# A 31-tap depthwise convolution on VectorE, written as three half-length filters on even and odd tokens

## The chip, the cores and the metric

The kernel runs on one core of one Trainium2 chip. The metric is the device time of one execution in microseconds (us), the median of several. Before the change it is 2021.61 us, the median of three runs (2020.27 to 2026.67).

## What is computed

The program is one step of a two-layer decoder trunk for 528 prompt tokens (16 learned ones and 512 given ones) and 8 sample tokens. Each layer is FFN, mixer, FFN, each with a root-mean-square norm ahead of it; the first layer's mixer is a convolution branch beside windowed attention, the second's a state-space scan. The change lies in the convolution branch, for the prompt tokens alone. Cut to that, the reference is:

```python
z = proj[..., o3:o4] * jax.nn.sigmoid(proj[..., o4:])          # 512 channels
zf = jnp.concatenate([ctx, z], axis=1)                         # 30 rows of zeros, then 528 tokens
y = lax.conv_general_dilated(zf, conv_w[:, None, :], (1,), 'VALID',
                             feature_group_count=C_CONV) + conv_b   # 31 taps for each channel
c_out = silu(layernorm(y, ln_g, ln_b))                         # over the 512 channels
out = jnp.concatenate([a_out, c_out], axis=-1) @ w_out         # a_out: the attention's output
```

## The kernel before

Channels lie on the 128 partitions and tokens along the free dimension; all is 32-bit. A tile of 536 columns holds two halves of 268: 264 prompt tokens and 4 sample tokens each. Every matrix product is done in three passes with high and low parts (`whi`, `wlo` of the weights, `xh`/`xl` or `mh`/`ml` of the operand), so a product with K blocks of 128 is 3 x K x 2 matmuls of 268 columns, and each block of weights costs a copy on ScalarE (L128) and a subtraction on VectorE (L129).

The mixer (`_mixer0`, from L508) has 512 convolution channels in four groups c = 0 to 3. For each, `z_tile(c)` computes the gated input with two products and leaves it in `zp[c]`, 30 zeros and then 528 tokens. `conv(c)` then multiplies `zp[c]`, shifted by j, with the weight column of tap j and adds it into `yc[c]`, one VectorE instruction of 528 columns for each tap (L573 the first, L575 the others). Group 3 is special: its first 8 taps (`NPE`) are done on TensorE as products with diagonal matrices (`conv_pe`, L587 to L594) into an accumulator `self.pc`; VectorE does the other 23, and L799 adds `self.pc` in. Each group has a `yc[c]` of its own and no other scratch.

When all four are there, `norm(h)` does the layer norm over channels for each half h: the mean by four products with a constant matrix (L778), the subtraction (L782), squares on ScalarE (L784), four products (L785), a reciprocal square root with one correction step (`rsqrt`, L297 to L302), the scaling (L790), Silu with scale and bias (L791) and the split into `mh[4+c]`, `ml[4+c]` (L148, L149). `project` then applies the output weights in two sweeps over eight groups d of output channels: first the attention half (24 matmuls for each d, L139 and L142, and the addition into `x[d]` on VectorE, L832), then the convolution half (24 more, L841). The next FFN follows.

The order on each engine is not the order of the text. A scheduler with a model of the chip's timing takes instructions in the text's order of priority as soon as what they read and the tiles they write are to be had, and so fills one step's gaps with another's work. A tile of a pool with `bufs=n` is given out anew when the last use of an older one in the text is over. The accumulators named `mm` (`acc2`) are two; `self.pc` is one of them, from `conv_pe` until L799 has read it.

Of the kernel before, what the change touches and what calls it, by code (L numbers as in the profile page):

```python
# [12 lines left out]
AF = mybir.ActivationFunctionType  # L13
OP = mybir.AluOpType
# [6 lines left out]
NP = 528  # L21
HP = 264
HT = 268
# [3 lines left out]
NCK = 66  # L27
NEG = -1e9
ORDER0 = "z0 k v q0 a0 z3 q1 a1 c0 z1 q2 a2 q3 z2 l s a3".split()
NCV, NPE = 3, 8  # L30
LOENG = lambda nc: nc.vector
SLOTS = dict(P1=0, P2=1, P6=3, P5=5, P7=6, P4=9, P3=11)
CHUNKS = ((0, 6), (6, 8), (14, 8))
WHOLE, HEAD = 3, tuple((d,) for d in range(8))
ORDER1 = [(a[0], int(a[1])) for a in
          "U0 U1 U2 U3 X0 X1 U4 X2 Y0 U5 X3 T0 U6 Y1 X4 T1 Y2 X5 T2 U7 Y3 X6 T3 Y4 Y5 X7 T4 Y6 T5 Y7 T6 T7".split()]

# [1 line left out]
def halves(ap):  # L39

    return ap.rearrange("p (h t) -> p h t", h=2)


def pv(ap):

    return halves(ap)[:, :, :HP]
# [7 lines left out]
def h2(ap):  # L54

    return ap.rearrange("p (h t) -> p h t", h=2)
# [6 lines left out]
class Trunk:  # L63
# [467 lines left out]
    def _mixer0(self, p, stage):  # L531
        nc, io, out, ident = self.nc, self.io, self.out, self.ident
        R = halves(self.R[:])
        win = io["ab_w_in"][0].rearrange("(k p) f -> p k f", p=128)
        cos, sin, perm, gmask, sel, maskb, mask4, identb, sk, sk4, sks, o512, cw, zs, sc, kcT, vc = (
            self.m0[n] for n in "cos sin perm gmask sel maskb mask4 identb sk sk4 sks o512 cw zs sc kcT vc".split())

        def tl(shape, name, dt=F32, bufs=1):
            return p.tile(shape, dt, name=name, bufs=bufs)

        wcol = lambda c, j: cw[:, c * 31 + j:c * 31 + j + 1]
        vcol = lambda i, c: cw[:, 124 + 4 * i + c:124 + 4 * i + c + 1]


        zp = [tl([128, 30 + NP], f"zp{c}") for c in range(4)]
        yc = [tl([128, NT], f"yc{c}") for c in range(4)]
# [18 lines left out]
            nc.vector.scalar_tensor_tensor(sv(yc[c][:]), zn, wcol(c, 30), sc[:, c].rearrange("p (h b) -> p h b", h=2),  # L565
                                           op0=OP.mult, op1=OP.add)

        def conv(c, hs=(0, 1), j0=0):
            y = halves(yc[c][:])[:, hs[0]:hs[-1] + 1, :HP]
            for j in range(j0, 31):  # L570
                z = h2(zp[c][:, j:j + NP])[:, hs[0]:hs[-1] + 1]
                if j == j0:
                    nc.vector.tensor_scalar(y, z, wcol(c, j), vcol(0, c), op0=OP.mult, op1=OP.add)  # L573
                else:
                    nc.vector.scalar_tensor_tensor(y, z, wcol(c, j), y, op0=OP.mult, op1=OP.add)  # L575

        def conv_pe(i):

# [195 lines left out]
        def norm(h):  # L774
            hc = slice(h * HT, (h + 1) * HT)
            pm = self.bank()[:, :HT]
            for c in range(4):
                nc.tensor.matmul(pm, o512[:], yc[c][:, hc], start=c == 0, stop=c == 3)  # L778
            pq = self.bank()[:, :HT]
            for c in range(4):  # L780
                y = yc[c][:, hc]
                nc.vector.tensor_sub(y, y, pm)  # L782
                s = self.work("ta")[:, :HT]
                nc.scalar.activation(s, y, AF.Square)  # L784
                nc.tensor.matmul(pq, o512[:], s, start=c == 0, stop=c == 3)  # L785
            rl = self.R[:, hc]
            self.rsqrt([rl], [pq])
            for c in range(4):
                y = yc[c][:, hc]
                nc.vector.tensor_mul(y, y, rl)  # L790
                nc.scalar.activation(y, y, AF.Silu, scale=vcol(1, c), bias=vcol(2, c))  # L791
                self.put(self.mh[4 + c][:, hc], self.ml[4 + c][:, hc], y)

        for c in range(WHOLE):
            conv(c)
        if NPE < 31:
            conv(3, j0=NPE)
            y = pv(yc[3][:])
            nc.vector.tensor_add(y, y, self.pc[:, :, :HP])  # L799
        else:  # L800
            nc.scalar.activation(pv(yc[3][:]), self.pc[:, :, :HP], AF.Identity, bias=vcol(0, 3))
        for h in range(2):
            for c in range(WHOLE, NCV):
                conv(c, (h,))
            norm(h)

        pz = self.bank()
# [657 lines left out]
```

## Time and profile before

| | before |
|---|---|
| median of 3 runs | 2021.61 us |
| the profiled execution | 2020.43 us |
| its span, first to last instruction | 2018.6 us |
| TensorE busy, mean granted clock | 1933.7 us, 0.984 |
| VectorE busy | 1577.0 us |
| ScalarE busy | 938.1 us |

Busy time counts an instruction from its start to its end; matmuls overlap, so a full busy time says only that TensorE was never empty. How many matmuls were done in a stretch, and the granted clock beside them, say more. A row of the timeline that merges several instructions gives the start of the first and the time from there to the end of the last.

### The profile page before, as it was taken

What the parts mean: (1) busy time and instruction counts of PE and PEld (TensorE: products, weight loads), DVE (VectorE), ACT (ScalarE), POOL (GpSimd) and SP (SyncE); (2) the same over time, 40 slices, a digit from 0 to 9 for tenths busy, and PEclk for the clock granted to TensorE, in tenths of its full rate; (3) what the DMA queues carried; (4) which work ended last, traced back from release to release, by engine and by line L of the source; (5) the groups of instructions that cost most, each with busy time, mean ns of one, the idle gap of its engine ahead of it and who ended that gap; (6) DMA issues with size and microseconds to landing.
All of it is one profiled execution on the core that took longest, in us unless ns stands there. A gap on an engine that the chain in (4) does not pass through costs nothing.

```text
span 2018.6 us, 37789 instructions
## 1 busy us (share of the span) xinstructions
PE 1933.7 (96%) x15338; PEld 1870.4 (93%) x15338; DVE 1577.0 (78%) x2799; ACT 938.1 (46%) x1639; POOL 81.4 (4%) x160
## 2 busy tenths in 40 slices
PE   6999999999999899999999999999989999999998
PEld 5999999998779899898999999999989999999997
DVE  5768769678868999989789997696694486794876
ACT  5535435434446635435465354354324364452543
POOL 2000000000000000020001210000110000000000
PEclk9899999999989999999999999999999999999999
DMA  6233333321005234353334543236583323333231
GB/s 185 81 107 87 95 95 95 116 75 44 27 22 123 65 94 127 121 156 113 102 94 120 163 130 103 86 102 193 164 261 101 90 63 95 95 111 89 84 105 53
DMA packets 372066, 213.51 MB, mean 106 GB/s; under 512 B 36299, under 2 KB 362503, under 8 KB 371869
## 3 DMA queue, kind: packets, MB, share of 16 engines
q1 hardware_dynamic: 354901, 190.63, 32.8%
q0 software_dynamic: 6432, 19.40, 3.0%
q10 hardware_dynamic: 10560, 1.09, 0.4%
q8 instruction: 120, 1.97, 0.4%
q14 instruction: 53, 0.43, 0.1%
HBM read 193.14 MB, written 23.65 MB: 107 GB/s over the span
## 4 chain that ended last, share of the span: by engine, by line
PE 73%; DVE 14%; DMA 5%; issue 4%; ACT 3%; ACTq 0%; POOL 0%; SPq 0%; DVEq 0%; POOLq 0%
PE mm L266 25%; PE mm L139 18%; PE mm L142 9%; PE S L139 7%; PE S L266 4%; PE S L142 4%; DMA raw<-in_ffn_w_gu 3%; DVE wlo L225 2%; PE S L747 1%; ACT whi L128 1%; DVE ml L149 1%; DVE wlo L129 1%; DVE ql L225 1%; DMA pb<-in_x_prompt 1%; DVE raw L229 1%
## 5 line engine op out<-in xcount | busy, mean ns | idle before, releaser
L224 ACT ACTIVATE whi<-raw 128x1024 fp32r<-128x1024 f32 (+1 forms) x237 | 216.9, 916 | 184.1 <-PE mm L266 50.5
L128 ACT ACTIVATE whi<-raw 128x1024 fp32r<-128x1024 f32 (+2 forms) x166 | 159.6, 973 | 303.3 <-PE mm L139 156.7
L139 PE MATMUL mm<-mh,whi 128*128 128x268 f32 x1224 | 262.1, 291 | 5.9 <-ACT whi L128 3.0
L225 DVE TENSOR_TENSOR wlo<-raw,whi 128x1024 fp32r<-128x1024 f32 (+1 forms) x237 | 246.7, 1041 | 25.5 <-ACT whi L224 24.7
L139 PE MATMUL mm<-ml,whi 128*128 128x268 f32 x1224 | 259.5, 287 | 0.1
L142 PE MATMUL mm<-mh,wlo 128*128 128x268 f32 x1224 | 259.5, 288 | 0.1
L129 DVE TENSOR_TENSOR wlo<-raw,whi 128x1024 fp32r<-128x1024 f32 (+2 forms) x166 | 184.5, 1117 | 70.1 <-ACT whi L128 67.7
L139 PEld LDWEIGHTS mm<-mh,whi 128*128 128x128 f32 x1224 | 194.5, 190 | 10.6 <-ACT whi L128 4.1
L142 PEld LDWEIGHTS mm<-mh,wlo 128*128 128x128 f32 x1224 | 194.5, 189 | 1.6 <-DVE wlo L129 1.2
L139 PEld LDWEIGHTS mm<-ml,whi 128*128 128x128 f32 x1224 | 194.9, 189 | 0.7 <-DVE ml L149 0.4
L266 PE MATMUL mm<-xh,whi 128*128 128x268 f32 x632 | 183.6, 291 | 5.9 <-ACT sn L274 5.3
L266 PE MATMUL mm<-eh,wlo 128*128 128x268 f32 x632 | 181.5, 287 | 3.2 <-DVE wlo L225 3.2
L266 PE MATMUL mm<-eh,whi 128*128 128x268 f32 x632 | 182.4, 289 | 1.8 <-ACT whi L224 1.1
L266 PE MATMUL mm<-xh,wlo 128*128 128x268 f32 x632 | 181.0, 286 | 0.0
L266 PE MATMUL mm<-xl,whi 128*128 128x268 f32 x632 | 180.8, 286 | 0.0
L266 PE MATMUL mm<-el,whi 128*128 128x268 f32 x632 | 180.6, 286 | 0.0
L266 PEld LDWEIGHTS mm<-xh,whi 128*128 128x128 f32 x632 | 119.0, 188 | 10.6 <-ACT sn L274 9.6
L139 PE MATMUL S<-mh,whi 128*128 128x268 f32 x568 | 121.3, 289 | 3.0 <-ACT mh L148 1.6
L266 PEld LDWEIGHTS mm<-eh,wlo 128*128 128x128 f32 x632 | 118.8, 188 | 4.2 <-DVE wlo L225 4.0
L266 PEld LDWEIGHTS mm<-eh,whi 128*128 128x128 f32 x632 | 119.1, 188 | 3.6 <-ACT whi L224 1.6
L142 PE MATMUL S<-mh,wlo 128*128 128x268 f32 x568 | 120.1, 287 | 0.3 <-DVE wlo L129 0.3
L266 PEld LDWEIGHTS mm<-xl,whi 128*128 128x128 f32 x632 | 119.1, 189 | 0.0
(520 smaller groups left out, 5079.7 us busy)
## 6 DMA issues: line engine op xcount, KB each, us to landing
raw<-in_ffn_w_gu SPq DMA_DIRECT2D x174, 512.0 KB
raw<-in_ffn_w_down SPq DMA_DIRECT2D x64, 512.0 KB
raw<-in_ffn_w_down SPq DMA_DIRECT2D x32, 384.0 KB
raw<-in_ssm_w_glu SPq DMA_DIRECT2D x16, 512.0 KB
raw<-in_ab_w_in SPq DMA_DIRECT2D x10, 512.0 KB
dB<-B POOLq DMA_DIRECT2D x16, 256.0 KB, 2.9
dC<-Z POOLq DMA_DIRECT2D x32, 128.0 KB, 3.2
dT<-dK POOLq DMA_DIRECT2D x8, 512.0 KB, 5.0
```

The lines of the kernel that those rows point to most:

```text
L128: nc.scalar.activation(hi[:, :K], raw[:, :K], AF.Copy)
L129: nc.vector.tensor_sub(lo[:, :K], raw[:, :K], hi[:, :K].bitcast(F32))
L139: nc.tensor.matmul(ps[:, h, :HT], hi[:, k, :], src[:, h * HT:(h + 1) * HT], start=(k == 0 and i == 0), stop=False)
L142: nc.tensor.matmul(ps[:, h, :HT], lo[:, k, :], xh[k][:, h * HT:(h + 1) * HT], start=False, stop=(k == K - 1))
L149: nc.vector.tensor_sub(lo, src, hi.bitcast(F32))
L224: nc.scalar.activation(h, r, AF.Copy)
L225: nc.vector.tensor_sub(l, r, h.bitcast(F32))
L229: nc.vector.tensor_add(U[:, k0], U[:, k0], G[:, k0])
L266: nc.tensor.matmul(ps, w[:, c + k, :], b[k], start=bool(first and k + i == 0), stop=bool(last and k == 3 and i == 2), skip_group_check=True)
L747: nc.tensor.matmul(S[:, g, :w], qT[t][rw, 128 * b:128 * b + 128], kT[rw, k0:k0 + w], start=False, stop=True)
```

## The change

Even and odd outputs are computed apart. With z1 the odd tokens, d0 = even - odd and d1 = next even - odd, the 31-tap sum for the even outputs is S + (16 taps on d0), for the odd ones S + (15 taps on d1), where S is 16 taps on z1 with the sums of neighbouring weights (`ws`). Each of the three filters runs on 264 columns. For a group that is two subtractions, 16 + 16 + 15 instructions in place of 31; for group 3, whose first 8 taps stay on TensorE, 12 + 12 + 11 in place of 23. `z1` is read with a step of two elements, and the last instruction of each phase writes `yc[c]` with a step of two. S and the running sum y lie in the two halves of `self.sq`, a tile that the norms of the FFNs use and that is free here; d0 and d1 are one tile each. All four groups use the same S, y, d0 and d1. `conv(3)` stands last in the text, as before.

```diff
-NCV, NPE = 3, 8
+NPE = 8
-WHOLE, HEAD = 3, tuple((d,) for d in range(8))
+HEAD = tuple((d,) for d in range(8))
...
-        def conv(c, hs=(0, 1), j0=0):
-            y = halves(yc[c][:])[:, hs[0]:hs[-1] + 1, :HP]
-            for j in range(j0, 31):
-                z = h2(zp[c][:, j:j + NP])[:, hs[0]:hs[-1] + 1]
-                if j == j0:
-                    nc.vector.tensor_scalar(y, z, wcol(c, j), vcol(0, c), op0=OP.mult, op1=OP.add)
+        ws = tl([128, 4, 16], "ws")
+        cwv = cw[:, :124].rearrange("p (c j) -> p c j", c=4)
+        nc.vector.tensor_add(ws[:, :, :15], cwv[:, :, 0:30:2], cwv[:, :, 1:31:2])
+        nc.vector.tensor_copy(ws[:, :, 15], cwv[:, :, 30])
+
+        def conv(c, j0=0):
+
+            z, n, i0 = zp[c], HP + 15, j0 // 2
+            d0, d1 = (tl([128, n], name)[:] for name in ("d0", "d1"))
+            z1 = z[:, 1:2 * n:2]
+            S, y = self.sq[:, :HP], self.sq[:, HT:HT + HP]
+            nc.vector.tensor_sub(d0, z[:, 0:2 * n:2], z1)
+            nc.vector.tensor_sub(d1[:, :n - 1], z[:, 2:2 * n:2], z1[:, :n - 1])
+            for i in range(i0, 16):
+                w = ws[:, c, i:i + 1]
+                if i == i0:
+                    nc.vector.tensor_scalar(S, z1[:, i:i + HP], w, vcol(0, c), op0=OP.mult, op1=OP.add)
                 else:
-                    nc.vector.scalar_tensor_tensor(y, z, wcol(c, j), y, op0=OP.mult, op1=OP.add)
+                    nc.vector.scalar_tensor_tensor(S, z1[:, i:i + HP], w, S, op0=OP.mult, op1=OP.add)
+            for p, (d, last) in enumerate(((d0, 15), (d1, 14))):
+                o = halves(yc[c][:])[:, :, p:HP:2]
+                for i in range(i0, last + 1):
+                    a, b, t = d[:, i:i + HP], y if i > i0 else S, y
+                    if i == last:
+                        a, b, t = h2(a), h2(b), o
+                    nc.vector.scalar_tensor_tensor(t, a, wcol(c, 2 * i + p), b, op0=OP.mult, op1=OP.add)
...
-        for c in range(WHOLE):
+        for c in range(3):
             conv(c)
...
```

What is left out are branches that were not taken and the same calls in other words. In the changed kernel L582 and L583 write d0 and d1, L587 and L589 are the taps of S, L596 the taps of the two phases, L819 the addition of `self.pc`; L803 to L812 are the norm, L848 and L857 the additions into `x[d]`.

The first place is VectorE, from the last taps of group 3 to the first of group 1. Before (`yc3` is group 3, `mm_5389` is `self.pc`, `zp1` the input of group 1):

```order
L575 SCALAR_TENSOR_TENSOR yc3_4629<-zp3_4625,cw_1467,yc3_4629 128x2x264
L560 SCALAR_TENSOR_TENSOR ta_5558<-mm_5448,R_117 128x536
L575 SCALAR_TENSOR_TENSOR yc3_4629<-zp3_4625,cw_1467,yc3_4629 128x2x264
L562 SCALAR_TENSOR_TENSOR zp1_4623<-tb_5559,ta_5558 128x528
L564 SCALAR_TENSOR_TENSOR zs_1574<-tb_5559,ta_5558 128x8
L129 TENSOR_TENSOR wlo_5813<-raw_5811,whi_5812 128x1024
L666 TENSOR_REDUCE st_5368<-S_5361 128x2
L149 TENSOR_TENSOR ml1_110<-ms_5324,mh1_102 128x128
L575 SCALAR_TENSOR_TENSOR yc3_4629<-zp3_4625,cw_1467,yc3_4629 128x2x264
L573 TENSOR_SCALAR yc1_4627<-zp1_4623,cw_1467 128x2x264
L565 SCALAR_TENSOR_TENSOR yc1_4627<-zs_1574,cw_1467,sc_1575 128x2x4
L799 TENSOR_TENSOR yc3_4629<-yc3_4629,mm_5389 128x2x264
```

Group 3 is done, and `self.pc` read, as group 1 begins. In the changed kernel VectorE has no tap of group 3 there; these are the end of group 2 and of group 3 in it, with the additions of the attention half's products (L848) between the taps (`mm_5392` is `self.pc`):

```order
L596 SCALAR_TENSOR_TENSOR yc2_4628<-d1_6240,cw_1467,sq_118 128x2x132
L583 TENSOR_TENSOR d1_6291<-zp3_4625 128x278
L596 SCALAR_TENSOR_TENSOR sq_118<-d0_6290,cw_1467,sq_118 128x264 x3
L848 TENSOR_TENSOR x2_79<-mm_6504,x2_79 128x536
...
L596 SCALAR_TENSOR_TENSOR sq_118<-d1_6291,cw_1467,sq_118 128x264 x3
L596 SCALAR_TENSOR_TENSOR yc3_4629<-d1_6291,cw_1467,sq_118 128x2x132
L848 TENSOR_TENSOR x6_83<-mm_6636,x6_83 128x536
L819 TENSOR_TENSOR yc3_4629<-yc3_4629,mm_5392 128x2x264
L129 TENSOR_TENSOR wlo_6739<-raw_6737,whi_6738 128x512
L803 TENSOR_TENSOR yc0_4626<-yc0_4626,ms_6330 128x268
```

Group 3 now comes last, behind group 2, whose S, y, d0 and d1 it takes over, and seven of the eight additions of the attention half stand ahead of L819.

The second place is TensorE, in the attention half of the projection. Before, with `mm_6359` and `mm_6392` the accumulators of d = 0 and d = 1:

```order
L139 MATMUL mm_6359<-mh0_101,whi_6361 128x268 x2
L139 MATMUL mm_6392<-mh0_101,whi_6394 128x268 x2
L139 MATMUL mm_6359<-ml0_109,whi_6361 128x268 x2
L142 MATMUL mm_6359<-mh0_101,wlo_6362 128x268 x2
L139 MATMUL mm_6359<-mh1_102,whi_6361 128x268 x2
L139 MATMUL mm_6392<-ml0_109,whi_6394 128x268
```

Two of them are open at once. After, `mm_6438`, `mm_6471` and `mm_6504` are d = 0, 1 and 2:

```order
L799 MATMUL ms_6330<-yc1_4627,o512_1275 128x268
L139 MATMUL mm_6438<-mh3_104,whi_6440 128x268
L139 MATMUL mm_6438<-ml3_112,whi_6440 128x268 x2
L142 MATMUL mm_6438<-mh3_104,wlo_6441 128x268 x2
L139 MATMUL mm_6471<-mh0_101,whi_6473 128x268 x2
...
L142 MATMUL mm_6471<-mh3_104,wlo_6474 128x268 x2
L139 MATMUL mm_6504<-mh0_101,whi_6506 128x268 x2
```

One product is finished before the next begins, for all eight d, and the products of the mean (L799, L778 before) stand among them: those of group 3's `yc` behind the last.

## Rows read from the trace of the kernel before

**Rows 1.** Page, busy time, share of the span and instructions
```profile
PE 1933.7 (96%) x15338; PEld 1870.4 (93%) x15338; DVE 1577.0 (78%) x2799; ACT 938.1 (46%) x1639; POOL 81.4 (4%) x160
```
**Rows 2.** Windows: start:end, length, busy (x count) of PE PEld DVE ACT POOL, PEclk
```profile
410.00:430.00 20.00, 20.00 (x161) 19.86 (x160) 13.06 (x22) 9.07 (x12) 0.00 (x0) 1.00 0.31 79
510.00:541.00 31.00, 31.00 (x228) 27.07 (x226) 25.89 (x49) 11.12 (x35) 0.00 (x0) 1.00 0.11 31
541.00:587.00 46.00, 39.56 (x210) 26.82 (x210) 37.17 (x79) 20.36 (x75) 0.00 (x0) 0.70 0.02 7
587.00:618.00 31.00, 30.89 (x223) 29.12 (x222) 22.14 (x51) 21.42 (x40) 0.55 (x1) 1.00 0.23 64
618.00:643.00 25.00, 22.33 (x166) 21.90 (x166) 19.53 (x45) 15.20 (x25) 0.00 (x0) 0.93 0.77 158
```
**Rows 3.** Tile yc: durations in ns (min/median/max), first and last start
```profile
L575 DVE SCALAR_TENSOR_TENSOR yc<-zp,cw,yc x112: 744/760/771, 433.6 to 582.3; 128x528 f32<-128x528 f32 x112
L784 ACT ACTIVATE ta<-yc x8: 411/414/429, 589.2 to 605.3; 128x268 f32<-128x268 f32 x8
L148 ACT ACTIVATE mh<-yc x8: 408/410/413, 603.3 to 617.2; 128x268 fp32r<-128x268 f32 x8
L149 DVE TENSOR_TENSOR ml<-yc,mh x8: 426/433/439, 603.7 to 617.9; 128x268 fp32r<-128x268 f32 x8
L799 DVE TENSOR_TENSOR yc<-yc,mm x1: 693/693/693, 509.8 to 509.8; 128x528 f32<-128x528 f32 x1
```
**Rows 4.** Timeline, VectorE: taps of one group; a chain of 268 columns
```profile
488.56 2.37 DVE L575 SCALAR_TENSOR_TENSOR yc<-zp,cw,yc 128x528 f32<-128x528 f32 x3
610.03 0.44 DVE L300 SCALAR_TENSOR_TENSOR tb<-ms,tb 128x268 f32<-128x268 f32 x1
610.50 0.30 DVE L301 TENSOR_SCALAR tb<-tb 128x268 f32<-128x268 f32 x1
```
**Rows 5.** Timeline: one accumulator handed on between the two products of group 1
```profile
493.29 0.37 PE L142 MATMUL mm<-xh,wlo 128*128 128x268 f32 x1
493.81 0.70 DVE L557 TENSOR_TENSOR tb<-mm,R 128x536 f32<-128x536 f32 x1
494.57 0.63 PE L139 MATMUL mm<-xh,whi 128*128 128x268 f32 x2
```
**Rows 6.** Critical chain: a tap in it; attention's last product, the first mean
```profile
558.49 0.72 DVE yc L575
585.99 0.67 PE ms L761 x8
586.66 2.00 PE ms L778 x8
```
**Rows 7.** Timeline: an addition into x and a low part of weights
```profile
607.80 0.72 DVE L832 TENSOR_TENSOR x<-mm,x 128x536 f32<-128x536 f32 x1 [0.38 <-PE mm L142]
608.43 0.68 DVE L129 TENSOR_TENSOR wlo<-raw,whi 128x512 fp32r<-128x512 f32 x1
```
**Rows 8.** Timeline, ScalarE in the norm
```profile
609.04 0.49 ACT L297 ACTIVATE ta<-ms,eps 128x268 f32<-128x268 f32 x1
609.43 0.57 ACT L811 ACTIVATE ta<-ms 30x512 f32<-30x512 f32 x1
612.36 1.28 ACT L791 ACT_TABLE_LOAD   x1
613.66 1.11 ACT L791 ACTIVATE yc<-yc,cw 128x268 f32<-128x268 f32 x2
```
**Rows 9.** Timeline: the convolution half, half-clock matmuls, the FFN's first
```profile
625.29 0.63 ACT L128 ACTIVATE whi<-raw 128x512 fp32r<-128x512 f32 x1 [7.73 <-DMA craw<-in_ssm_c_re]
628.35 0.43 PE L142 MATMUL mm<-mh,wlo 128*128 128x268 f32 x1
628.57 0.42 PE L139 MATMUL mm<-mh,whi 128*128 128x268 f32 x1
642.94 0.42 PE L139 MATMUL S<-xh,whi 128*128 128x268 f32 x2
```

More of the change, by code (lines that the diff above doesn't have):

```diff
@@ L792, in norm @@
                 self.put(self.mh[4 + c][:, hc], self.ml[4 + c][:, hc], y)
-        for c in range(WHOLE):
+        for c in range(3):
             conv(c)
[L796 to L801, printed above, removed]
+        conv(3, j0=NPE)
+        y = pv(yc[3][:])
+        nc.vector.tensor_add(y, y, self.pc[:, :, :HP])
         for h in range(2):
-            for c in range(WHOLE, NCV):
-                conv(c, (h,))
             norm(h)
```

## The prediction

> **What bounds the kernel now.** The page comes first: TensorE is busy for 96% of the span, VectorE for 78% [rows 1]. So a microsecond saved on VectorE counts only where TensorE waits for it. Next comes the place of the convolution: its taps start between 433.6 and 582.3 us [rows 3], inside a mixer that ends, for this purpose, when the next FFN's first matmul starts at 642.94 [rows 9]. The windows cut that stretch into stages [rows 2]. To 541, TensorE does 228 matmuls in 31 us at full clock; in the undisturbed stretch 410 to 430 it does 161 in 20, that is 0.124 us for one of 268 columns. From 541 to 587 it does 210 in 46 us at a mean granted clock of 0.70: the last attention heads are a chain over three engines. From 587 to 618 it is full again, at clock 1.00: it does the attention half of the projection while VectorE and ScalarE do the norm. That is the cover that the change touches. Here the convolution is over in time: the last tap starts at 582.3, and attention's last product is followed at 586.66, without a gap, by the products of the mean [rows 6]. The norm's last low part starts at 617.9 and takes 0.43 [rows 3].
>
> **The price of a tap.** Three taps of one group in a row take 2.37 us; with 0.76 for the last, that is 0.80 from start to start, since each needs the sum that the one before it wrote [rows 3, 4]. For 264 columns the nearest rows are a dependent chain of 268: 0.44 us for one, 0.47 from start to start [rows 4]. An input with a step of two elements appears in no row; bounds are 0.44 (as the dense row) and 0.80 (as if the skipped columns were read too). I take 0.47, the row of the same width. Then a group of 31 taps goes from 30 x 0.80 + 0.6 = 24.6 us to (47 + 2) x 0.47 = 23.0, group 3 from 22 x 0.80 + 0.6 = 18.2 to (35 + 2) x 0.47 = 17.4. Together VectorE saves 3 x 1.6 + 0.8 = 5.6 us, for 21% fewer columns but 58% more instructions in a group of 31 (49, with the two subtractions). The two instructions for `ws` are of 60 and 4 columns; they stand in the first FFN, where TensorE is full, and I cost them at nothing (0.5 us if it were not).
>
> [...]
>
> **What moves, and the wait that this adds.** Before, the four groups had nothing in common, so group 3's taps ran early beside group 0's, and L799 released `self.pc` at 509.8 + 0.69 = 510.5 [rows 3]. Now all groups share S, y, d0 and d1, and group 3 stands last in the text. So it waits for group 2, whose input is the last that TensorE delivers. Two things follow.
>
> First, `self.pc` keeps one of the two `mm` accumulators for some 100 us longer. Each product there must then wait until VectorE has emptied the one before. Such a handing on stands in the trace from when both kernels have one: the last matmul starts at 493.29, the VectorE instruction at 493.81, the next product at 494.57 [rows 5], so 1.28 us from start to start instead of 0.124, some 1.15 lost where no attention work fills it. In q2, q3 and z2 attention does fill it, except for about 2 us behind q2 (two VectorE instructions, a product, two more), with 1 us for the rest: 3 us.
>
> Against this stand the attention's waits. A tap in front of a small instruction holds it up; one such tap is a piece of 0.72 us of the chain that ended last [rows 6]. With 0.44 in place of 0.76, the mean wait behind a tap falls by 0.16; over some 20 VectorE steps of the last heads that is 3 us, and group 3's 17 us no longer compete earlier. Also some 5 us of attention's products move ahead of z2's end as filler, and leave the tail. I take attention's end 3 us earlier, at 583.7, with bounds of 7 us earlier (all waits shrink) and 1 us later (the handing on is not filled).
>
> **The norm loses its cover.** Behind attention's last product VectorE's order still has 43 tap and subtraction instructions ahead of L819, with 7 additions into x (0.71), 6 low parts (0.68) and L819 itself (0.69): 43 x 0.47 + 5.0 + 4.1 + 0.7 = 30.0 us [rows 3, 4, 7]. Some of the taps alternate between two groups and may run closer, at 0.40 by the ratio of width, which gives 27. TensorE needs about as long for the attention half: 24 x 0.124 = 3.0 us for each d, then 0.38 + 0.72 + 0.1 for the addition [rows 7], 4.2 us together, some 26 for the six and a bit that L819 waits for. So L819 ends at about 583.7 + 30 = 613.7, and by then the attention half is all but done.
>
> Only now can the last product of the mean be made, and the norm runs with TensorE nearly empty. To its first reciprocal root it takes 5.9 us: a product (0.5), a subtraction, the squares, with the second half's four products (2.0, as [rows 6]) queued ahead of the last two products of the squares. From there ScalarE works without a gap: 4 squares 1.5, table load 1.28, three Silu and a copy and a Silu 2.6, table load 1.28, root 0.49, two evacuations 1.2, three copies 1.2, table load 1.28, four Silu with four copies 3.8, which is 14.6 [rows 3, 8]. So the norm's last part is in place at 613.7 + 20.5 = 634.2. Before it was at 618.3. If each hand-over costs 0.3 us more than I have put, it is 24 instead of 20.5; 18 if the halves overlap better.
>
> From there to the FFN's first matmul was 24.6 us before: ScalarE issues the transfers for the state-space weights, which holds the next weights' copy up by 7.73 us, then come five d of 24 matmuls, some at half clock (0.22 us from start to start) [rows 9]. ScalarE's queue is the same here, so I leave the 24.6 as it is, and the first FFN matmul comes at 658.8 in place of 642.9.
>
> **Sum.** The delay is 30.0 + 20.5 - (618.3 - 586.7) = +18.9, less 3 for attention's end: +16. Nothing behind changes. On the profiled execution's 2020.43 (span 2018.6 and 1.8 around it) that is 2036.4; the median before is 1.2 above the profiled one, so 2037.6, say 2038.
>
> **Rivals.**
> *The clock falls as well.* Before, 587 to 618 was at clock 1.00 and 541 to 587, with its sparse matmuls, at 0.70 [rows 2]. [...] Against it: before, the engine also fell there, and 166 matmuls still fit into the 25 us from 618. At the full price it gives 2056; I give 0.15 to more than 2048.
> *The step of two is not free.* If the taps on z1 take 0.80, the 12 of group 3 and what is left of group 2 cost 12 x 0.33 = 4 us behind attention and some 5 before: 2045. For it speaks only that no row shows such a read; 0.07. [...]
> *The delay is absorbed.* Attention ends 7 us early, the taps behind it run at 0.40 and the norm in 18: 27 + 18 - 31.6 - 7 = +6, and a little more gives no change (within 0.3%, 6 us, about what a measurement of this kernel tells from none): 2024. For it: VectorE was busy for 37.2 of the 46 us of the tail [rows 2]. 0.13.
> *Faster.* If short taps free the attention tail itself, the place is 541 to 587: VectorE would have to finish groups 2 and 3 before attention ends, which decides from the point where under 8 us of taps are left behind it. Then the old cover is whole again, the tail gains 3 to 7 us and the time is 2016. Against it is the order, which puts 43 tap instructions behind attention's last. That the change doesn't do what it says, and VectorE gains nothing at all, belongs to the forecast, which rests on 5.6 us hardly at all. 0.05.
>
> **How the numbers follow.** The forecast has 0.60, its own range 2030 to 2045: +9 to +24 from the bounds of attention's end, of the taps left (27 to 30) and of the norm (18 to 24). With the rivals, 8 in 10 lie between 2025 and 2050. Faster 0.05; same 0.13; slower 0.60 + 0.15 + 0.07 = 0.82.
>
> **What will show it.** L589 and L596 at 0.43 to 0.45 us each; L819 near 613 where L799 was at 509.8; gaps of about 1.2 us between the attention half's products; a window of some 20 us behind L819 with few matmuls; the last L149 of the norm near 634, the FFN's first matmul near 659; the same distance from there to the end. It is wrong if L819 comes before 600, or if the norm ends within 7 us of 618.

## The result, and the profile after

The changed kernel takes 2048.45 us (median of four runs, 2045.68 to 2051.08) where the kernel before takes 2022.09 (2020.27 to 2026.67): 1.0125 times as long (95% interval 1.0104 to 1.0147), and the two medians are 26.4 us apart. The forecast was slower, 2038, with a range of its own of 2030 to 2045: the direction came, and the time lies 3 us above that range. The profiled execution took 2050.56 us with a span of 2048.6, 30.0 above the span of before, at a mean granted clock of 0.983 against 0.984. Page, busy time:

```profile
PE 1940.6 (95%) x15338; PEld 1874.4 (91%) x15338; DVE 1578.4 (77%) x2869; ACT 940.5 (46%) x1639; POOL 81.8 (4%) x160
```

VectorE has 70 instructions more than in [rows 1] and is busy 1.4 us longer, not 5.6 us less. Groups of VectorE's instructions from 430 to 612 us: line, operation, tiles and shapes, count, busy us, mean ns, idle before:

```profile
L596 DVE SCALAR_TENSOR_TENSOR sq<-d,cw,sq 128x264 f32<-128x264 f32 x108 | 52.8, 489 | 1.7
L589 DVE SCALAR_TENSOR_TENSOR sq<-zp,ws,sq 128x264 f32<-128x264 f32 x56 | 27.3, 488 | 0.8
L583 DVE TENSOR_TENSOR d<-zp 128x278 f32<-128x278 f32 x4 | 1.8, 443 | 0.0
```

A short tap takes 0.49 us, with a dense input (L596) as with one read in steps of two (L589). Tile `yc`, the rows that answer to [rows 3]:

```profile
L596 DVE SCALAR_TENSOR_TENSOR yc<-d,cw,sq x8: 485/494/496, 461.9 to 608.0; 128x264 f32<-128x264 f32 x8
L149 DVE TENSOR_TENSOR ml<-yc,mh x8: 427/430/439, 624.8 to 634.6; 128x268 fp32r<-128x268 f32 x8
L819 DVE TENSOR_TENSOR yc<-yc,mm x1: 693/693/693, 609.5 to 609.5; 128x528 f32<-128x528 f32 x1
```

The addition of `self.pc`, at 509.8 before, starts at 609.5; the norm's last low part, at 617.9 before, at 634.6. The windows, against [rows 2]:

```profile
510.00:541.00 31.00, 27.75 (x202) 21.36 (x200) 26.52 (x62) 13.64 (x42) 0.00 (x0) 1.00 0.07 18
590.00:620.00 30.00, 24.20 (x159) 21.42 (x159) 22.13 (x45) 7.67 (x14) 0.00 (x0) 0.98 0.20 57
620.00:650.00 30.00, 22.80 (x134) 20.36 (x133) 17.90 (x49) 20.92 (x38) 0.55 (x1) 0.83 0.43 73
```

From 590 to 620 TensorE does 159 matmuls; before it did 223 in the 31 us from 587. ScalarE is busy for 7.7 us of these 30: until the last group is summed it has only copies of weights to do. TensorE's timeline in that stretch:

```profile
576.42 1.13 PE L782 MATMUL ms<-pT,vtok 128*64 128x128 f32 x8 [0.69 <-ACT pT L777]
577.48 2.16 PE L799 MATMUL ms<-yc,o 128*128 128x268 f32 x4
...
597.41 0.48 PE L139 MATMUL mm<-mh,whi 128*128 128x268 f32 x2 [0.90 <-DVE x L848]
601.53 0.48 PE L139 MATMUL mm<-mh,whi 128*128 128x268 f32 x2 [0.90 <-DVE x L848]
605.64 0.48 PE L139 MATMUL mm<-mh,whi 128*128 128x268 f32 x2 [0.90 <-DVE x L848]
609.76 0.48 PE L139 MATMUL mm<-mh,whi 128*128 128x268 f32 x2 [0.90 <-DVE x L848]
...
612.70 0.61 PE L799 MATMUL ms<-yc,o 128*128 128x268 f32 x2
...
614.29 1.17 PE L806 MATMUL ms<-ta,o 128*128 128x268 f32 x4 [0.86 <-ACT ta L805]
...
658.78 0.42 PE L139 MATMUL S<-xh,whi 128*128 128x268 f32 x2
```

Attention's last product starts at 576.42. From 593 on each d of the attention half takes 4.1 us and begins only when VectorE has added the one before into `x` (the bracket: 0.90 us idle, released by L848). VectorE in its turn waits for the product that it is to add, since the addition stands between the taps in its order:

```profile
592.43 0.72 DVE L848 TENSOR_TENSOR x<-mm,x 128x536 f32<-128x536 f32 x1 [1.90 <-PE mm L142]
596.55 0.72 DVE L848 TENSOR_TENSOR x<-mm,x 128x536 f32<-128x536 f32 x1 [0.41 <-PE mm L142]
```

Seven of the eight products are added ahead of L819. The eighth, from 609.76, holds the norm up: the mean's last products (L799), which L819 releases at 610.2, stand behind it on TensorE and start at 612.70. Behind 614 TensorE has little to do but the norm's own products. The FFN's first matmul comes at 658.78, 15.84 later than in [rows 9].

### The profile page after: what moved, and what is told of

It is laid out like the page before. It is cut to its first block, busy times and chain, and to the rows that moved or that the text cites. A ratio compares the mean times of both kernels' runs of the same rounds, so it can differ in the third digit from the quotient of the medians.

```text
span 2048.6 us, 37878 instructions
## 1 busy us (share of the span) xinstructions
PE 1940.6 (95%) x15338; PEld 1874.4 (91%) x15338; DVE 1578.4 (77%) x2869; ACT 940.5 (46%) x1639; POOL 81.8 (4%) x160
## 4 chain that ended last, share of the span: by engine, by line
PE 74%; DVE 14%; DMA 5%; issue 4%; ACT 3%; ACTq 0%; DVEq 0%; POOL 0%; SPq 0%
PE mm L266 24%; PE mm L139 19%; PE mm L142 9%; PE S L139 8%; PE S L266 4%; PE S L142 4%; DMA raw<-in_ffn_w_gu 3%; DVE wlo L225 2%; PE S L768 1%; DVE ml L149 1%; ACT whi L128 1%; DVE wlo L129 1%; DVE ql L225 1%; DVE tb L286 1%; DMA pb<-in_x_prompt 1%
## 5 line engine op out<-in xcount | busy, mean ns | idle before, releaser
L225 DVE TENSOR_TENSOR wlo<-raw,whi 128x1024 fp32r<-128x1024 f32 (+1 forms) x237 | 246.9, 1042 | 26.4 <-ACT whi L224 25.2
L139 PE MATMUL S<-ml,whi 128*128 128x268 f32 x568 | 119.7, 287 | 0.0
## 6 DMA issues: line engine op xcount, KB each, us to landing
raw<-in_ffn_w_down SPq DMA_DIRECT2D x32, 384.0 KB
```

What stands on the lines that cost most here:

```text
L139: nc.tensor.matmul(ps[:, h, :HT], hi[:, k, :], src[:, h * HT:(h + 1) * HT], start=(k == 0 and i == 0), stop=False)
L225: nc.vector.tensor_sub(l, r, h.bitcast(F32))
```

## The experiments

Each stands beside runs of the kernel before on the same chip: 2019.95 us (17 runs) for the first four, 2021.61 (7 runs) for the others. All are given in one table at the end of this section.

**The changed kernel again**, unchanged.

> The changed kernel once more, for a second trace of the same instruction order. Theory A (the delay is made in the mixer and by the other order that the scheduler chose up to 1009 us; behind that both kernels have the same order and the rest is scatter): the FFN's first matmul again within 1.5 us of 658.8, and the stretch from the second rstd (1071.8 in the first trace) to the end within 3 us of the kernel before, so the first trace's 7 us there are scatter. Rival (something lasting, such as the clock, makes the later stages longer in the changed kernel): the 7 us come again.

2050.38 us, ratio 1.0147 (1.0126 to 1.0168), span 2049.3. The loss repeats, and its places do too: the FFN's first matmul at 660.38, 0.1 us outside the 1.5 that were expected. From the norm of the next FFN to the end it takes 976.2 us, after 976.8 in the first trace and 970.8 in the kernel before: the excess there comes again, as the rival had it, and the theory of scatter fails. (The kernel before, profiled again below, has 975.4 there.) Attention's last product moved from 576.42 to 579.90 between the two executions, so about 3 us of it is chance.

**Group 3 second in the text**, with the new taps and the shared scratch kept.

```diff
-        for c in range(3):
-            conv(c)
+        conv(0)
         conv(3, j0=NPE)
         y = pv(yc[3][:])
         nc.vector.tensor_add(y, y, self.pc[:, :, :HP])
+        conv(1)
+        conv(2)
```

> The changed kernel with group 3 and the addition of self.pc second in the text (0, 3, 1, 2 in place of 0, 1, 2, 3), all else the same: the same 184 instructions, the same shared scratch. Theory A (group 3's place behind group 2 costs the time): no taps behind attention, L819's counterpart near 510 to 520, the norm's last low part at 616 +- 5, the FFN's first matmul at 641 +- 5, the whole 2014 to 2026. Rival B (more and shorter instructions on VectorE cost it, wherever they stand): 2040 or more. Rival C (half of the loss is the scheduler's other order behind the mixer, which has nothing to do with group 3): 2028 to 2038.

2023.79 us, 12 runs, ratio 1.0011 (0.9998 to 1.0025): the loss is gone. Tile `yc` in it:

```profile
L149 DVE TENSOR_TENSOR ml<-yc,mh x8: 426/434/439, 602.7 to 616.9; 128x268 fp32r<-128x268 f32 x8
L818 DVE TENSOR_TENSOR yc<-yc,mm x1: 696/696/696, 517.4 to 517.4; 128x528 f32<-128x528 f32 x1
```

With all 184 short instructions in place, but `self.pc` added at 517.4, the norm ends at 617.3, a microsecond before [rows 3]. The new form itself costs nothing that can be measured, and it gives nothing.

**The old taps with a shared sum.** The kernel before, with the running sum of all four groups in `self.sq` and only the last tap writing `yc[c]`.

```diff
+            s = pv(self.sq[:])
...
-                    nc.vector.scalar_tensor_tensor(y, z, wcol(c, j), y, op0=OP.mult, op1=OP.add)
+                    nc.vector.scalar_tensor_tensor(s if j < 30 else y, z, wcol(c, j), s, op0=OP.mult, op1=OP.add)
```

> The kernel before with its own taps of 528 columns, but with the running sum of all groups in one tile (self.sq), the last tap of each group writing its yc: 116 tap instructions as before, group 3 behind group 2 as in the changed kernel. Theory A: slower, as the changed kernel; 29 taps of 0.80 are left behind attention, 23 us, with 10 us of other VectorE work: the FFN's first matmul at 655 to 665, the whole 2036 to 2052. Rival B (the shorter taps cost the time): within 6 us of the kernel before.

2047.60 us, ratio 1.0138 (1.0121 to 1.0156): the whole loss, without one short tap. Its `yc`:

```profile
L576 DVE SCALAR_TENSOR_TENSOR yc<-zp,cw,sq x4: 769/769/772, 477.1 to 611.3; 128x528 f32<-128x528 f32 x4
L149 DVE TENSOR_TENSOR ml<-yc,mh x8: 428/432/439, 626.0 to 635.9; 128x268 fp32r<-128x268 f32 x8
L800 DVE TENSOR_TENSOR yc<-yc,mm x1: 705/705/705, 612.1 to 612.1; 128x528 f32<-128x528 f32 x1
```

**The held accumulator given back.** The changed kernel, with `self.pc` copied by ScalarE into `ml[7]` right behind `conv_pe` and added from there; that copy has the type of the high parts (`fp32r`), and the low part of group 3's first 8 taps is left out.

```diff
+            nc.scalar.activation(pv(self.ml[7][:]), self.pc[:, :, :HP], AF.Copy)
...
-        nc.vector.tensor_add(y, y, self.pc[:, :, :HP])
+        nc.vector.tensor_add(y, y, pv(self.ml[7][:].bitcast(F32)))
```

> The changed kernel with self.pc copied out of its accumulator by ScalarE as soon as it is complete (into a tile that is free until the norm, in the rounded 32-bit format of the high parts, so the low bits of group 3's first 8 taps are lost), and added from there at the end. Both accumulators are free from about 485 us on; group 3 still comes last. Theory A1 (the late group 3 itself and the norm without cover are the cause): the gaps between the attention half's products go, but the norm's last part comes at 628 to 636 and the whole is 2036 to 2049. Rival A2 (the held accumulator is the cause): within 8 us of the kernel before.

2047.83 us, ratio 1.0129 (1.0106 to 1.0151). The loss stays; the norm's last low part comes 2.0 us earlier:

```profile
L149 DVE TENSOR_TENSOR ml<-yc,mh x8: 427/432/440, 622.7 to 632.6; 128x268 fp32r<-128x268 f32 x8
L820 DVE TENSOR_TENSOR yc<-yc,ml x1: 709/709/709, 607.4 to 607.4; 128x528 f32<-128x528 f32 x1
```

The gaps do go: a d now takes 2.97 us instead of 4.12, as VectorE's additions show.

```profile
593.35 0.72 DVE L849 TENSOR_TENSOR x<-mm,x 128x536 f32<-128x536 f32 x1 [0.32 <-PE mm L142]
596.32 0.72 DVE L849 TENSOR_TENSOR x<-mm,x 128x536 f32<-128x536 f32 x1 [0.32 <-PE mm L142]
```

But attention's last product starts at 583.20, 3 to 7 us later than in the two profiles of the changed kernel, and the norm's last low part comes only 2.0 us earlier than in the first of them and 4.1 earlier than in the second. So the accumulator's longer life is worth some 2 to 4 us there, not the loss.

**Group 3 alone in the old form**, in its place at the end of the text; groups 0 to 2 keep the new form.

```diff
             z, n, i0 = zp[c], HP + 15, j0 // 2
+            if c == 3:
+                y = halves(yc[c][:])[:, :, :HP]
...
+                        nc.vector.scalar_tensor_tensor(y, z, wcol(c, j), y, op0=OP.mult, op1=OP.add)
+                return
```

> The changed kernel, with group 3's 23 taps on VectorE in the old form: 528 columns each, summed in yc[3], without the shared S, y, d0 and d1; groups 0 to 2 keep the new form, and the text's order is unchanged. Theory A (the time is lost because group 3 has to wait for group 2's scratch, so that the norm comes behind the attention half): group 3 is done early again, self.pc is read before 530 us, the norm's last low part is in place at 615 to 620, the next FFN's first matmul at 640 to 645, and the time is that of the kernel before, 2016 to 2027. Rival B (the many short instructions of groups 0 to 2 cost the time, wherever group 3 stands): 139 of the 174 short taps are still there, so most of the loss stays: 2038 or more.

2017.46 us, ratio 0.9990 (0.9966 to 1.0015), no change. Group 3 needs nobody's scratch and the scheduler takes it early, though it stands last in the text; tile `yc` and the window against the one above:

```profile
L585 DVE SCALAR_TENSOR_TENSOR yc<-zp,cw,yc x22: 755/760/769, 468.5 to 506.4; 128x528 f32<-128x528 f32 x22
L149 DVE TENSOR_TENSOR ml<-yc,mh x8: 426/434/439, 601.4 to 615.5; 128x268 fp32r<-128x268 f32 x8
L605 DVE SCALAR_TENSOR_TENSOR yc<-d,cw,sq x6: 473/484/494, 462.2 to 583.6; 128x264 f32<-128x264 f32 x6
L828 DVE TENSOR_TENSOR yc<-yc,mm x1: 700/700/700, 508.3 to 508.3; 128x528 f32<-128x528 f32 x1
```
```profile
590.00:620.00 30.00, 29.89 (x231) 28.96 (x230) 21.53 (x58) 19.31 (x35) 0.55 (x1) 1.00 0.37 84
```

231 matmuls in the 30 us in which the changed kernel does 159. That is the cover, back again. (The expectation miscounts: with the first tap of each sum there are 176 short taps in the changed kernel, and 141 of them are left here; its two theories stay apart all the same.)

**Fewer taps in the last place.** `conv(3, j0=28)` in place of `conv(3, j0=NPE)` in the changed kernel: taps 8 to 27 of group 3 are left out.

> The changed kernel with the taps 8 to 27 of group 3 left out, so that group 3 issues 5 tap instructions and 2 subtractions on VectorE instead of 35 and 2; it still comes last and shares the scratch. 30 instructions of 0.50 us are 15 us less between attention's end and L819. Theory A: L819 ends near 595 instead of 610, and the norm's last low part is in place at 618 to 622 instead of 635, the FFN's first matmul near 644. From there two theories part. If what is lost later (14 us of the 30 in the profiled executions: 6 to 8 in the two FFNs behind, 4 in the state-space mixer, 2 at the end) comes with a late mixer, it goes as well: 2020 to 2028. If it comes with the changed code itself, it stays: 2031 to 2037.

2030.23 us, ratio 1.0047 (1.0024 to 1.0071), where the changed kernel has 1.0125 and 1.0147, each against the kernel before on its own chip: 16 to 20 us less, for 15 us of work taken from that place.

```profile
L149 DVE TENSOR_TENSOR ml<-yc,mh x8: 430/436/439, 611.7 to 624.2; 128x268 fp32r<-128x268 f32 x8
L819 DVE TENSOR_TENSOR yc<-yc,mm x1: 692/692/692, 592.2 to 592.2; 128x528 f32<-128x528 f32 x1
```

L819 comes 17.3 us earlier, the last low part 10.4: the norm now takes 31.7 us behind L819, since its products share TensorE with the attention half again (215 matmuls from 590 to 620 us). The time, 2030, is just below the range of the theory in which the later loss stays (2031 to 2037) and above that in which it goes (2020 to 2028): some of it stays. The table says where.

**The kernel before again.**

> The kernel before, unchanged, for a second profile of it. The state-space mixer took 198.0 us in the first profile of it and 197.8 in the kernel with group 3 second, but 201.8 to 203.8 in the four kernels with a late norm, with the same instructions in the same order and short stretches at half clock in it. If the half clock there comes with the late norm: 198 again and one stretch at most. If it is chance from one execution to the next: any value from 198 to 204. The time is 2012 to 2026.

2022.78 us, one run. The state-space mixer takes 202.4 us in it instead of 198.0. Windows of 60 us, from 37.3 us behind the start of that mixer, in the kernel before, in this run of it, and in the changed kernel, in that order:

```profile
1473.90:1533.90 60.00, 52.34 (x540) 50.28 (x540) 50.05 (x104) 20.45 (x40) 6.23 (x17) 0.97 0.73 215
```
```profile
1471.00:1531.00 60.00, 51.21 (x500) 49.08 (x501) 49.89 (x104) 18.46 (x36) 6.31 (x17) 0.91 0.70 209
```
```profile
1500.00:1560.00 60.00, 51.41 (x504) 49.48 (x505) 49.96 (x104) 19.06 (x37) 6.42 (x17) 0.91 0.70 210
```

The first profile of the kernel before had a granted clock of 0.97 and 540 matmuls there, its second one 0.91 and 500, as the changed kernel has. Some 4 us of the 30.0 between the two profiled executions are thus chance, in the clock, and not the change.

**A stall that both kernels have.** In the kernel before, the transfers of the state-space weights, issued on ScalarE's queue right behind the norm ([rows 9], 7.73 us), go to GpSimd's queue: `nc.gpsimd.dma_start` for `nc.scalar.dma_start` in six lines.

> The kernel before with the 22 transfers that fetch the state-space weights issued on GpSimd's queue in place of ScalarE's. In the kernel before and in the changed one ScalarE's next weight copy waits 7.73 and 6.80 us behind those issues, between the norm and the next FFN. If that stall holds up TensorE, the FFN's first matmul comes up to 7 us earlier (636 to 640) and the time is 2012 to 2017, below both kernels. If the convolution half and its weights set the start anyway: no change, 2018 to 2023. If GpSimd, which also issues the later transfers of that preparation, becomes late with them: 2025 or more.

2020.12 us, ratio 1.0001 (0.9977 to 1.0025), no change. ScalarE's and TensorE's timelines:

```profile
614.88 0.61 ACT L128 ACTIVATE whi<-raw 128x512 fp32r<-128x512 f32 x1
619.06 1.25 ACT L128 ACTIVATE whi<-raw 128x512 fp32r<-128x512 f32 x2 [2.93 <-PE mm L139]
```
```profile
636.79 0.42 PE L139 MATMUL S<-xh,whi 128*128 128x268 f32 x2
```

The stall is gone and the FFN starts 4.6 us (against the second profile of before) to 6.2 us earlier, as the first theory had it, but the median does not show it. Its profiled execution had one of the long state-space mixers (203.1 us, as the table shows). A saving of 4.6 us is just inside the interval, which reaches to 0.9977, and is not shown; the kernel does not beat the one before by a measured margin.

The stages of all profiled executions, in us, each from one landmark to the next: the FFN's first matmul, then the first product of the sum of squares (L310) in each of the next three stages' norms.

| kernel | FFN's first matmul | that FFN | next FFN | state-space mixer | rest | span |
|---|---|---|---|---|---|---|
| before | 642.9 | 404.9 | 388.7 | 198.0 | 384.0 | 2018.6 |
| before, again | 641.3 | 404.3 | 388.1 | 202.4 | 384.9 | 2021.0 |
| before, transfers moved | 636.8 | 404.4 | 389.8 | 203.1 | 384.2 | 2018.3 |
| group 3 in the old form | 639.6 | 404.6 | 389.7 | 198.3 | 384.7 | 2016.9 |
| group 3 second | 641.1 | 408.1 | 387.1 | 197.8 | 382.2 | 2016.3 |
| fewer taps last | 647.9 | 410.3 | 387.8 | 200.0 | 383.6 | 2029.6 |
| accumulator given back | 656.8 | 411.3 | 390.9 | 203.8 | 385.0 | 2047.7 |
| old taps, shared sum | 659.9 | 411.3 | 389.7 | 201.8 | 383.7 | 2046.4 |
| changed | 658.8 | 413.0 | 391.0 | 201.9 | 384.0 | 2048.6 |
| changed, again | 660.4 | 412.7 | 390.4 | 202.1 | 383.7 | 2049.3 |

Mean of the two profiles of the changed kernel less mean of the two of before: +17.5 up to the FFN's first matmul, +8.2 in that FFN, +2.3 in the next, +1.8 in the state-space mixer, -0.6 behind it, together 29.2. The mixer's times scatter over early (197.8 to 203.1 us) and late kernels (200.0 to 203.8), and so do the next FFN's (387.1 to 389.8, and 387.8 to 391.0), so in these two no effect of the change can be told from the scatter. The 8.2 in the FFN can: the five kernels with a late norm have 410.3 to 413.0, the others 404.3 to 408.1.

What that FFN loses can be read only in part, and no run takes it apart. All five have another order of VectorE's instructions there, since the scheduler gives its filler, the preparation of the state-space weights, to other gaps. At equal distance from the FFN's first matmul (160 to 180 us), first the changed kernel, then before:

```profile
818.80:838.80 20.00, 16.18 (x123) 15.10 (x122) 20.00 (x39) 9.98 (x16) 0.00 (x0) 1.00 0.20 59
```
```profile
802.90:822.90 20.00, 18.81 (x150) 18.39 (x149) 20.00 (x52) 10.32 (x18) 0.00 (x0) 1.00 0.28 82
```

VectorE is busy for all of the 20 us in both, and the clock is 1.00 in both, but the changed kernel does 27 matmuls fewer, some 3.3 us at 0.124 each. The longest of TensorE's waits in that stretch, us in total, times, longest, in the changed kernel and before:

```profile
PE mm L266 <- DVE wlo L225: 1.8, 1, 1.8
```
```profile
PE mm L266 <- DVE wlo L225: 0.9, 1, 0.9
```

This place is not common to the five: with the old taps and a shared sum, where the FFN takes 411.3 us, the same stretch has 151 matmuls. First that kernel there; then, 20 to 40 us behind the FFN's first matmul, the changed kernel and before:

```profile
819.92:839.92 20.00, 19.52 (x151) 18.59 (x149) 20.00 (x49) 10.94 (x21) 0.00 (x0) 1.00 0.28 81
```
```profile
678.78:698.78 20.00, 14.25 (x94) 13.58 (x95) 20.00 (x75) 14.60 (x31) 0.00 (x0) 0.74 0.09 27
```
```profile
662.94:682.94 20.00, 15.21 (x101) 14.52 (x102) 20.00 (x66) 14.68 (x32) 0.00 (x0) 0.83 0.19 54
```

The second stretch loses 7 matmuls more, with a lower granted clock. The rest of the 8 us is not traced. With group 3 in the old form that FFN also has an order of its own, and loses nothing, so another order alone does not cost this. Whether the late start or the order that comes with it makes the 8 us stays open.

## Why the prediction was right, and where it was not

**The mechanism.** Shown from both sides. Short taps without the move (group 3 second) and with group 3 out of the sharing give no loss; the move without short taps (old taps, shared sum) gives all of it. The point named as deciding, the place of group 3 behind attention's end, and the norm that loses the projection as its cover, is what the runs turn on. The forecast of slower, 2038, was right in direction and mechanism; the measured 2048.45 lies above its own range of 2030 to 2045, inside the wider one with the rivals (2025 to 2050).

**The price of a tap.** Taken as 0.44 us for one and 0.47 from start to start; measured 0.49, and 0.53 from start to start (three in a row take 1.55). The row I had taken it from, L300, has a constant where a tap has a column of weights. In the kernel before the same excess stands between such pairs of one operation: 0.760 for the old taps of 528 columns [rows 3] against 0.703 for L562 with a constant, and 0.770 for L158, with a column, against 0.710 for L286, with a constant, at 536. It is not in the width alone: the subtraction of 278 columns (L583) takes 443 ns, a tap of 264 takes 488. With 49 x 0.53 = 26 us a group of 31 taps that follow each other takes longer than the 24.6 reckoned for before; taps of two groups in turn start 0.40 apart, as the prediction allowed (L589 and L596 from 576.13 to 579.97). Together the 5.6 us saved on VectorE came out as 1.4 us more. The forecast rested on them hardly at all.

**The step of two** cost nothing here, 488 ns (L589) against 489 (L596), so that rival falls.

**Attention's end** was put 3 us earlier than before; it came 5 to 10 us earlier, by two profiles of each kernel. The short taps alone are not why: with the old taps and a shared sum the last product starts at 579.49, with the short taps and group 3 second at 584.96. It is earlier in the kernels with group 3 last, but by how much varies: 583.20 with the accumulator given back, 581.45 with fewer taps. Which of the prediction's reasons makes it stays open.

**The norm without cover.** From attention's end to the end of L819 30.0 us were expected and 32.7 measured (577.5 to 610.2): 45 tap and subtraction instructions instead of 43, with seven additions and six low parts of weights as expected, and 3.5 us in which VectorE waits for a product of the attention half (1.90 once and 0.40 or 0.41 four times), for which the sum had no term. The norm was put at 20.5 us, 24 at most, and took 24.8 (610.2 to 635.0). To its first root it took 8.0 us (to 618.2) instead of 5.9, because the eighth product of the attention half stands ahead of the mean's last products: they start 2.5 us behind L819, where the sum had them at once. From the root it took 16.8 instead of 14.6; ScalarE did not work without a gap, as the sum had it. These two errors, +7.0 together, cancelled the one in attention's end (-6.2) and one of -0.8 behind the norm, and the FFN's first matmul stands at 658.78 where 658.8 was forecast. That this number was met so closely is luck; the terms were off by up to 6 us each.

**The step that failed** is "Nothing behind changes", and it is why the time lies above the forecast's range. Of the 30.0 us between the two profiled executions 14.1 lie behind the FFN's first matmul. Some 8 are real, in the very next FFN, where I had not looked: VectorE is full for 20 us at a time there, and the scheduler's order differs. Some 4 were chance in the state-space mixer's clock. By the medians, +26.4 instead of +16.

**The other rivals.** The measured time lies where the prediction had put its rival of a falling clock, above 2048, but not by that mechanism. No run shows the term behind that rival's full price, 2056; what the runs showed in its place is this, from the norm's last low part to the FFN's first matmul, first the changed kernel, then before:

```profile
635.00:658.78 23.78, 19.89 (x146) 19.40 (x145) 18.67 (x43) 14.96 (x24) 0.00 (x0) 0.93 0.78 159
```
```profile
618.30:642.94 24.64, 21.97 (x163) 21.54 (x162) 19.17 (x44) 15.14 (x25) 0.00 (x0) 0.93 0.77 160
```

The clock is 0.93 in both and the stretch is 0.9 us shorter, so nothing was added there. Some matmuls of the convolution half did run 0.22 us apart, at half clock, from 628 to 632 (the granted clock was 0.50 there, 0.83 in the mean from 620 to 650), but under the norm, whose last low part comes later. Of what an absorbed delay would have needed, attention ended early enough in the first profile, but VectorE's stretch took 32.7 us instead of 27 and the norm 24.8 instead of 18. And faster would have needed group 3 to be all but done by attention's end, where 45 instructions were left.

## What to carry to other kernels

Scratch that several independent groups share is an order between them: it takes from a scheduler the freedom to do first what arrives first, and that can cost far more than the instructions it was meant to save. Where a scratch must be shared, write the groups in the order in which their inputs come; here moving group 3's three lines up brought the time back to that of before (ratio 1.0011, 0.9998 to 1.0025). Look for what a stage covers before its input is made late, and look into the next stage too where the engine that feeds it is already full.

## What the runs showed beyond that

Two profiles of one unchanged kernel differed by 4.4 us in one stage of 200, with the same instructions in the same order: 540 matmuls at clock 0.97 in one, 500 at 0.91 in the other, over 60 us. A difference of a few us between single profiles, stage by stage, needs a second profile of the kernel before it is given a cause. And in these kernels an instruction with a factor from a column took some 0.05 us longer than one with a constant (0.49 against the 0.44 of [rows 4], 264 and 268 columns; 0.760 against 0.703 at 528), and the excess did not halve with the width: by estimate, from the 0.05, 8.6 us of VectorE over 172 short taps.
